# The attention mixers' task order taken from a table, and two weight splits of the Strassen stages issued earlier

## The chip, the core and the metric

One core of a Trainium2 chip runs the program. Its engines are TensorE (PE: matmuls and transposes, with weight loads that overlap them), VectorE (DVE), ScalarE (ACT), GpSimd (POOL) and SyncE (SP, which issues most of the DMAs). Each engine works through its own instructions in the order in which they were issued and waits at semaphores for the others. The metric is the device time of one execution in microseconds (us); less is better.

## The reference, cut to what matters

One decoder layer on x of 512 x 1024 (float32):

```
h  = x + 1/2 * SwiGLU_1(RMSNorm(x))                    # 1024 -> 2816 -> 1024
u  = RMSNorm(h);  one projection u @ w_in (3992 columns): q, k, v, gates
A  = NSA attention, 8 heads: compressed + selected + sliding window 512
B  = sliding-window attention (window 128), 8 heads, with a sink per head
h  = h + w_out(sigmoid(gA) * (A @ w_branch_a) + sigmoid(gB) * (B @ w_branch_b))
h  = h + 1/2 * SwiGLU_2(RMSNorm(h));   out = RMSNorm_final(h)
```

The compressed keys and values of NSA come from a small network: blocks of 32 tokens, 2048 -> 256, a tanh-GELU, 256 -> 64. With 512 tokens the selection takes all blocks of 64, so the selected branch is dense causal attention here.

## The kernel before, in words

**Numbers.** Each float32 operand is kept as two parts, a rounded high half and the rest as a low half, and a product is three matmuls (high x high, high x low, low x high). A weight block of 1024 x 128 is loaded by SP into a ring of raw tiles (`raw`, 4 deep) and split: `W.high`, line 160, copies the high half on ACT (`whi`), `W.low`, line 164, subtracts on DVE or POOL (`wlo`). The halves live in a ring of 4 slots, so a block's split may start when the block four places ahead is no longer read. `W.next()` hands out a block and first calls `W.prep` for the block two places on; `W.prep(n)` issues load and split of all blocks up to n that are still to be done.

**Stages.** First feed-forward part, mixers (about 387 to 652 us of the span), merge of the two branches and `w_out`, second feed-forward part. Instructions are issued to each engine in the order of the Python code, except in the mixers.

**The mixers.** Their work is 1123 tasks, made by `plan.add` and numbered in the order of their making. A task says which engine may run it and for how long by the planner's estimate (`us`; some have two engines, DVE or POOL), what it comes after, and which buffers it takes from a ring and gives back. `Schedule.run` is a list scheduler: it always issues the task that could start first by its own clocks, and so chooses the order on all engines and, for tasks with two engines, the engine. Fillers are projections and gate matmuls that keep PE at work between the attention's steps. Attention goes unit by unit: scores on PE (`s`), masked minimum on DVE (line 1261), exponentials on ACT (1269), reciprocal of the sum on DVE (1279), weighing of the probabilities on DVE or POOL (1290, 1292), transposes on PE (1355, `tp`), their two halves on ACT and DVE (1367, 1370), product with the values on PE (`o`).

At two places of the stage the tasks' numbers are needed; a p behind a number says POOL. Around 451 to 457 us the list scheduler issues

```
183 518 515 208 185 519 210 551 209 203 212 211 204 214 205 213 184 206 215 520 186 248 187 250
249p 521 216 252 217 532 254 251p 547 218 207 188 219
```

183, 515, 519, 551, 203 to 206 and 216 are PE's. 183 ends a projection of keys and values, 185 and 186 are its rotary products and their addition (line 893), 187 is the low half of its values (`v_low`, line 940), which frees the `acc` bank that 216, the first step of the next projection, takes. 209, 211, 213 and 215 are halves of splits (line 164). Around 474 to 490 us it issues

```
581 586 572 561 239 256 269 240 257 271 258 270p 259 273 558 275 272p 228 260 559 562 309 261 582
311 274p 563 313 277 315 262 278 276p 229 230 564 587 310p 573 263 279 231 574 280 264 312p 583
565 281 314p 265 575 588 584 603 266 316p 589 576
```

Here 239 ends a projection, 240 is its rotary products on DVE; 256 to 259 are the second half of the values' compression on PE; 260 adds its halves, 261 sums them on PE, 262 is the polynomial of the GELU (lines 1095 to 1098, DVE), 263 the tanh (ACT), 264 the product (lines 1105 and 1106, DVE), 265 the second matrix on PE. 581, 586 and 603 are scores of the window attention (0.48 us by the planner's formula), 282 is a step of a projection (0.725), 565 a sum of two halves of an attention output (line 1398, 0.84), 241 a rotary addition. 270, 272, 274, 276, 310, 312, 314 and 316 are halves of splits.

**The second feed-forward part.** 22 column blocks f in thirds of 8, 8 and 6. For each f there are two products, `pg` and `pu`, of 24 matmuls each; `gated` then forms silu(pg) * pu. In the first two thirds every odd f closes a pair, and `gated` goes on to form the seven sums that Strassen's scheme wants of the pair (lines 1503 to 1510), in their two halves. After a third, `down()` runs 14 steps of 12 matmuls (`STEPS`); each takes its weight block by `W.next()`, and each reads one of the seven sums, of the first two pairs (g = 0) or the last two (g = 1). The first four steps are (1, 0), (5, 0), (2, 0) and (1, 1); their banks are `acc`, `o`, `s` and `acc`. When `down()` begins, the blocks of the first two steps are split already, and that of the third is issued by the first step's `W.next()`.

Of the kernel before, what the change touches and what calls it, by code (L numbers as in the profile page):

```python
# [27 lines left out]
NEVER = 1e9  # L28
# [27 lines left out]
def f32(ap):  # L56
    return ap.bitcast(F32)


class Weights:  # L60
# [6 lines left out]
    def __init__(self, tc, ctx):  # L67
        self.nc = tc.nc
        self.raw_pool = ctx.enter_context(tc.tile_pool(name="wraw", bufs=self.RAW))
        pool = ctx.enter_context(tc.tile_pool(name="wring", bufs=1))  # L70
        self.hi = pool.tile([128, self.SLOTS, 8, 128], F32R, name="whi")
        self.lo = pool.tile([128, self.SLOTS, 8, 128], F32R, name="wlo")
        self.tc = tc
        self.blocks, self.wide = [], []
        self.stored = {}
        self.raw = []
        self.apart = {}
        self.prepped = 0
        self.pos = 0
# [109 lines left out]
    def next(self):  # L189
        i = self.pos  # L190
        self.prep(i + self.AHEAD)
        self.pos += 1
        return self.place(i)
# [25 lines left out]
    return dram(w, r0 * width + c0, [[width, 128], [128 * width, nk], [1, n]])  # L219


class Ring:


# [15 lines left out]
class Task:  # L240


    def __init__(self, us, emit, take, give, rank):
        self.us, self.emit, self.take, self.give, self.rank = us, emit, take, give, rank
        self.left, self.next, self.ready, self.sources = 0, [], 0.0, []


class Schedule:
# [10 lines left out]
    def add(self, us, emit, after=(), take=(), give=(), rank=0):  # L259

        t = Task(us, emit, take, give, rank)
        t.seq = len(self.tasks)
        for p in after:
            if p is not None:
                t.left += 1
                p.next.append(t)
        self.tasks.append(t)
        return t

    def delay(self, source, engine):  # L270
        return 0.0 if source == engine else self.SEM[source] + (self.TO_POOL if engine == "pool" else 0.0)

    def run(self):
        ready = [t for t in self.tasks if t.left == 0]
        for _ in self.tasks:
            best = None
            for t in ready:
                at = t.ready
                for ring, _ in t.take:
                    at = max(at, ring.ready())  # L280
                for e, us in t.us.items():
                    start = max(at, self.clock[e], self.port if "pool" in t.us else 0.0, *(end + self.delay(p, e) for p, end in t.sources))
                    key = (start, t.rank, us, t.seq)
                    if best is None or key < best[0]:
                        best = key, t, e, start + us
            _, t, e, end = best
            assert end < NEVER
            for ring, key in t.take:
                ring.take(key)
            for ring, key in t.give:  # L290
                ring.give(key, end)
            self.clock[e] = end
            if "pool" in t.us:
                self.port = end
# [11 lines left out]
def layer(ctx, tc, a, out):  # L306
# [5 lines left out]
    W = Weights(tc, ctx)  # L312
# [399 lines left out]
    with ExitStack() as mixing:  # L712
# [66 lines left out]
        plan = Schedule(act=3.0, dve=5.0)  # L779
# [3 lines left out]
        PREP, FILL, FETCH = -2, 9000, 5.0  # L783
        engine = {"dve": vector, "pool": gpsimd}
        fill = [None]
        used, prepped = {}, {}

        def task(engines, emit, after=(), **kw):
            if isinstance(engines, tuple):
                engines = {engines[0]: engines[1]}  # L790
            return plan.add(engines, emit, [x for x in after if x is not None], **kw)

        def either(us, more=0.06):

            return {"dve": us + more, "pool": 2 * us + 0.1}

        last_low = [None]

        def prepare(first, n):

            for half in range(2):
                for i in range(first, first + n):
                    if i in W.stored:
                        if half == 0:
                            prepped[i, 0] = prepped[i, 1] = task(("sp", FETCH), lambda i=i: W.fetch(i),
                                                                 (used.get(i - W.SLOTS),), rank=PREP)
                        continue
                    if i < W.prepped:
                        prepped[i, half] = None
                        continue  # L810
                    nk = W.blocks[i][1] // 2
                    k = slice(half * nk, half * nk + nk)
                    us = nk * 128 / 960 + 0.07
                    t = task(("act", us + 0.04), lambda i=i, k=k: W.high(i, k.start, k.stop), (used.get(i - W.SLOTS),),
                             rank=PREP)

                    def low(e, i=i, k=k, half=half):
                        W.low(i, k.start, k.stop, engine[e])
                        if half:
                            W.load(i + W.RAW)  # L820

                    x = prepped[i, half] = task(either(us, 0.12), low, (t, last_low[0] if half else None), rank=PREP)
                    if half:
                        last_low[0] = x

# [581 lines left out]
        nsa_count, swa_turns = [0], []  # L1407
        attend([*swa_units(0), *swa_units(1), *nsa_units(0), *nsa_units(1, (3, 2, 1, 0))])
        plan.clock["sp"] = plan.clock["store"] = 0.0
        plan.run()  # L1410
        W.pos = pos[0]
        W.prepped = pos[0] + 2
        att_stack.close()
# [50 lines left out]
    with pool("temp3", 2) as temp, pool("end") as end:  # L1464
# [18 lines left out]
        def gated(pg, pu, j, pairs):  # L1483
            z = temp.tile([128, S], F32, name="z")
            vector.tensor_tensor(z, pg, r_b, op=OP.mult)
            s = temp.tile([128, S], F32, name="s")
            scalar.activation(s, z, AF.Silu)
            t = temp.tile([128, S], F32, name="t")
            vector.tensor_tensor(t, pu, r_b, op=OP.mult)
            if not pairs:  # L1490
                g = temp.tile([128, 8, 256], F32, name="g").rearrange("p m c -> p (m c)")[:, :S]
                vector.tensor_tensor(g, s, t, op=OP.mult)
                split(G[:, j], G[:, 8 + j], g)
                return
            if j % 2 == 0:
                left["g"] = temp.tile([128, 8, 256], F32, name="g")
            g, p = left["g"], j // 2
            o = g[:, 1:3] if j % 2 else g[:, 0:8:7]
            vector.tensor_tensor(o, *(x.rearrange("p (i c) -> p i c", i=2) for x in (s, t)), op=OP.mult)
            if j % 2 == 0:  # L1500
                return
            hi, lo = left_hi[:, p], left["lo"][:, p]
            vector.tensor_tensor(g[:, 3], g[:, 7], g[:, 2], op=OP.add)
            scalar.copy(hi[:, 0:4], g[:, 0:4])
            vector.tensor_tensor(g[:, 4], g[:, 3], g[:, 0], op=OP.subtract)
            vector.tensor_tensor(lo[:, 0:4], g[:, 0:4], f32(hi[:, 0:4]), op=OP.subtract)
            vector.tensor_tensor(g[:, 5], g[:, 0], g[:, 7], op=OP.subtract)
            vector.tensor_tensor(g[:, 6], g[:, 1], g[:, 4], op=OP.subtract)
            scalar.copy(hi[:, 4:7], g[:, 4:7])
            vector.tensor_tensor(lo[:, 4:7], g[:, 4:7], f32(hi[:, 4:7]), op=OP.subtract)  # L1510
# [96 lines left out]
        for third, (f0, f1) in enumerate(THIRDS):  # L1607
            for f in range(f0, f1):
                pg = acc(False)
                mm3(pg, W.next(), u_in, KD, col if f == 0 else None)  # L1610
                pu = acc(False)
                mm3(pu, W.next(), u_in, KD, rows if f == 0 else None)
                if f < 2:
                    for d in range(4 * f, 4 * f + 4):
                        residual(d)
                if f == 1:
                    make_room()
                if third == 2:
                    next(last)
                gated(pg, pu, f - f0, third < 2)  # L1620
            if third < 2:
                down()
# [27 lines left out]
```

## Time and profile before

| | |
|---|---|
| median of 3 runs | 1136.74 us (1136.02 to 1137.89) |
| profiled execution, its own time | 1138.52 us |
| its span, first to last instruction | 1136.8 us |
| mean granted TensorE clock | 0.992 |
| PE busy | 1111.3 us, 98% of the span |
| DVE busy | 706.3 us, 62% |
| ACT busy | 472.0 us, 42% |
| POOL busy | 130.0 us, 11% |

Busy time of PE is the union of the matmuls' drawn lengths. Matmuls overlap in the pipeline: one of 256 columns is drawn 0.28 us long, and the next starts 0.12 us after it, so a short gap does not show as idle time. A granted clock of 1.00 is 2.4 GHz, 0.50 is 1.2 GHz. A row's bracket gives the idle time of the engine just before the instruction and what ended it; where an instruction waits for several things, the row names the one that came last by the profile, which can be another than the one that counted. "L164" is line 164 of the kernel before.

### The profile page before, as it was taken

The page shows a single profiled execution, that of the slowest core. Times are in us where ns is not written, and L with a number is a line of the kernel's source. Part 1 is how long each engine was busy: PE and PEld are TensorE (multiplying, and loading weights), DVE is VectorE, ACT ScalarE, POOL GpSimd, SP SyncE. Part 2 cuts the span into 40 slices and gives each one's busy share as a digit, 9 for nine tenths or more (in the row PEclk, how much of TensorE's full clock was granted, in tenths as well). Part 3 has the DMA queues.
Part 4 walks back from the last instruction along what each step waited for, and adds up shares of the span by engine and source line. Part 5 has one row for each costly group of instructions (what it writes and reads, how often), then busy time and mean ns, then how long its engine had stood idle before and what let it go on. Part 6 is the DMA issues. An engine that isn't in the chain of part 4 may idle for free.

```text
span 1136.8 us, 14825 instructions
## 1 busy us (share of the span) xinstructions
PE 1111.3 (98%) x5535; PEld 934.6 (82%) x5535; DVE 706.3 (62%) x1311; ACT 472.0 (42%) x887; POOL 130.0 (11%) x133
## 2 busy tenths in 40 slices
PE   7999999999999999989999999999999999999997
PEld 6888888888888999888888888788887888778875
DVE  4665447674656588888888645553656754675553
ACT  4443223321324457566666534443334322342332
POOL 0100000000002132731101233220000000000001
PEclk9999999999999999999999999999999999999999
DMA  7377657886734542224333245633243633264211
GB/s 228 93 240 227 199 165 241 286 275 212 241 125 140 147 111 76 75 75 144 116 122 111 88 144 165 169 99 87 84 126 120 189 85 101 75 195 138 82 67 74
DMA packets 201904, 163.16 MB, mean 144 GB/s; under 512 B 6820, under 2 KB 177384, under 8 KB 201832
## 3 DMA queue, kind: packets, MB, share of 16 engines
q1 hardware_dynamic: 199304, 158.00, 45.4%
q10 hardware_dynamic: 2528, 4.22, 1.0%
q8 instruction: 43, 0.70, 0.2%
q14 instruction: 29, 0.24, 0.1%
HBM read 133.88 MB, written 28.31 MB: 143 GB/s over the span
## 4 chain that ended last, share of the span: by engine, by line
PE 86%; DVE 5%; ACT 3%; DMA 2%; POOL 2%; issue 1%; SPq 0%; POOLq 0%; ACTq 0%; DVEq 0%
PE acc L328 34%; PE o L328 24%; PE s L328 24%; PE tp L1355 2%; DMA z<-zd 2%; DVE wlo L164 2%; POOL z L1453 1%; ACT whi L160 1%; POOL z L1431 1%; DVE s L1261 0%; PE tp L328 0%; DVE ml L332 0%; ACT mh L331 0%; DVE h L598 0%; ACT turn_a L516 0%
## 5 line engine op out<-in xcount | busy, mean ns | idle before, releaser
L164 DVE TENSOR_TENSOR wlo<-raw,whi 128x1024 fp32r<-128x1024 f32 (+2 forms) x194 | 214.3, 1136 | 33.2 <-ACT whi L160 33.1
L160 ACT CAST whi<-raw 128x1024 fp32r<-128x1024 f32 (+2 forms) x214 | 188.7, 917 | 98.0 <-PE acc L328 36.0
L328 PE MATMUL acc<-uh,whi 128*128 128x512 f32 x336 | 133.1, 396 | 0.0
L328 PE MATMUL acc<-ul,whi 128*128 128x512 f32 x336 | 131.3, 391 | 0.0
L328 PE MATMUL acc<-uh,wlo 128*128 128x512 f32 x336 | 131.2, 391 | 0.0
L328 PE MATMUL o<-uh,whi 128*128 128x512 f32 x264 | 104.3, 395 | 0.7 <-ACT uh L650 0.7
L328 PE MATMUL o<-ul,whi 128*128 128x512 f32 x264 | 103.2, 391 | 0.0
L328 PE MATMUL o<-uh,wlo 128*128 128x512 f32 x264 | 103.0, 390 | 0.0
L328 PE MATMUL s<-uh,whi 128*128 128x512 f32 x232 | 90.7, 391 | 0.0
L328 PE MATMUL s<-ul,whi 128*128 128x512 f32 x232 | 90.5, 390 | 0.0
L328 PE MATMUL s<-uh,wlo 128*128 128x512 f32 x232 | 90.5, 390 | 0.0
L328 PEld LDWEIGHTS acc<-uh,wlo 128*128 128x128 f32 x336 | 63.2, 188 | 14.0 <-DVE wlo L164 0.4
L328 PEld LDWEIGHTS acc<-ul,whi 128*128 128x128 f32 x336 | 63.3, 188 | 11.9
L328 PEld LDWEIGHTS acc<-uh,whi 128*128 128x128 f32 x336 | 63.3, 188 | 11.9
L328 PE MATMUL acc<-whi,uh 128*128 128x256 f32 x224 | 65.3, 292 | 2.0 <-DVE v L940 2.0
L328 PE MATMUL acc<-wlo,uh 128*128 128x256 f32 x224 | 64.1, 286 | 0.0
L328 PE MATMUL acc<-whi,ul 128*128 128x256 f32 x224 | 64.0, 286 | 0.0
L517 POOL TENSOR_TENSOR sqacc<-sqacc,turn_a 128x512 f32<-128x512 f32 x14 | 18.3, 1304 | 362.9 <-ACT turn_a L516 362.9
L328 PEld LDWEIGHTS o<-uh,whi 128*128 128x128 f32 x264 | 49.8, 189 | 11.9 <-ACT uh L650 1.1
L331 ACT CAST G<-g 128x512 fp32r<-128x512 f32 x28 | 17.4, 622 | 101.5 <-DVE g L569 72.3
L328 PEld LDWEIGHTS o<-uh,wlo 128*128 128x128 f32 x264 | 49.7, 188 | 10.6
L328 PEld LDWEIGHTS o<-ul,whi 128*128 128x128 f32 x264 | 49.9, 189 | 10.4
(339 smaller groups left out, 2306.3 us busy)
## 6 DMA issues: line engine op xcount, KB each, us to landing
raw<-in_ffn_gate_dram SPq DMA_DIRECT2D x42, 512.0 KB, 4.1
raw<-in_ffn_up_dram SPq DMA_DIRECT2D x42, 512.0 KB, 5.3
raw<-in_ffn_down_dram SPq DMA_DIRECT2D x34, 512.0 KB, 4.3
raw<-in_w_in_dram SPq DMA_DIRECT2D x20, 512.0 KB, 4.9
eraw<-in_ffn_down_dram SPq DMA_DIRECT2D x16, 512.0 KB, 6.5
raw<-t SPq DMA_DIRECT2D x16, 512.0 KB, 3.2
eraw<-in_w_in_dram SPq DMA_DIRECT2D x12, 512.0 KB, 7.1
early<-ehi SPq DMA_DIRECT2D x12, 512.0 KB, 5.2
```

What stands on the lines that cost most here:

```text
L160: self.nc.scalar.copy(self.place(i)[0][:, k0:k1], self.raw[i][:, k0:k1])
L164: engine.tensor_tensor(lo, self.raw[i][:, k0:k1], f32(hi), op=OP.subtract)
L328: tensor.matmul(out, lhsT, rhs, start=start, stop=stop)
L331: scalar.copy(hi, src)
L517: gpsimd.tensor_tensor(sqacc, sqacc, sq, op=OP.add)
L1355: tensor.transpose(ps[:w, hd], u.p[:, hd, kb * w:kb * w + w], ident)
L1431: gpsimd.tensor_tensor(z, z, r_b, op=OP.mult)
L1453: gpsimd.tensor_tensor(y, y, z, op=OP.add)
```

## The change

`Schedule` gets a second way to issue its tasks: `follow` reads a table, `ORDER`, with the numbers of all 1123 tasks in the order in which they are to be issued, with a p behind those that go to POOL. The tasks themselves are as before; that the second half of a split comes after the first half of the same block is now written down as a condition. In the second feed-forward part `W.prep` is called twice more at the end of each of the first two thirds: for the block of `down()`'s third step ahead of `gated` of the last f, and for that of the fourth step inside it, behind the product and ahead of the pair's sums. The diff, with the table cut to its first and last line and the two places named above:

```diff
+ORDER = """
+    0 1 2 3 4 5 6 7 14 15 16 10 11p 13 17 32 8 18 36 33 19 37 20 9 21 34 12 44 38 40 80 48 35 41 49 42 23 22 50 39p
...
+    513 528p 516 181 174 517 514 182 183 531 518 185 208 210 212 209 211 213 546 184 515 203 519 187 186p 204 205
+    214 551 520 206 547 216 521 217 248 215p 218 249p 188 252 192 219 220 250 253p 552 522 548 193 221 532 189 254
...
+    226 540 541 569 542 555p 236 570 543 237 227 238 571 544 545 556 557 560 239 572 561 256 269 240 257 258 271
+    270p 273 558 581 259 309 586 313 228 275 260 562 559 272p 261 311 274p 277 582 229 278 262 563 230 564 231 587
+    276p 263 279 280 565 312p 281 241p 310p 573 583 603 264 282 574 588 265 584 314p 283 608 266 604 267 605 284
+    585p 268 290 291 315 316p 566 285 567p 589 292 575 609 610 606 576 242 286 243p 577 293 294 288 295 611 296 578
...
+    458 473 474 475 476 477 478 479 468 1122p 480 469
+"""
...
-        self.left, self.next, self.ready, self.sources = 0, [], 0.0, []
+        self.left, self.next, self.after, self.ready, self.sources = 0, [], [], 0.0, []
...
                 p.next.append(t)
+                t.after.append(p)
...
+    def follow(self, order):
+
+        done = set()
+        for word in order.split():
+            t = self.tasks[int(word.rstrip("p"))]
+            e = "pool" if word[-1] == "p" else next(iter(t.us))
+            assert all(p in done for p in t.after) and all(ring.ready() < NEVER for ring, _ in t.take)
+            for ring, key in t.take:
+                ring.take(key)
+            for ring, key in t.give:
+                ring.give(key, 0.0)
+            done.add(t)
+            t.emit(e) if len(t.us) > 1 else t.emit()
+        assert len(done) == len(self.tasks)
...
-                    x = prepped[i, half] = task(either(us, 0.12), low, (t, last_low[0] if half else None), rank=PREP)
+                    x = prepped[i, half] = task(either(us, 0.12), low, (t, *((last_low[0], prepped[i, 0]) if half else ())), rank=PREP)
...
-        plan.run()
+        plan.follow(ORDER) if ORDER.strip() else plan.run()
...
             if j % 2 == 0:
                 return
+            if j == 7:
+                W.prep(W.pos + 3)
             hi, lo = left_hi[:, p], left["lo"][:, p]
...
                 if third == 2:
                     next(last)
+                if third < 2 and f + 1 == f1:
+                    W.prep(W.pos + 2)
                 gated(pg, pu, f - f0, third < 2)
```

Against the list scheduler's order no task of PE moves by more than 8 places among PE's own 444. 54 tasks change between DVE and POOL:

| kind of task | DVE to POOL | POOL to DVE |
|---|---|---|
| weighing of probabilities (1290, 1292) | 27 | 1 |
| low half of a split (164) | 7 | 2 |
| rotary addition (893) | 5 | 1 |
| low half of an attention output (1403) | 3 | 3 |
| low half of queries (972) | 2 | 1 |
| low half of the compression's input (1059) | 0 | 2 |

## Rows read from the trace of the kernel before

**Rows 1.** The page, part 1: busy us (share of span) xinstructions.

```profile
PE 1111.3 (98%) x5535; PEld 934.6 (82%) x5535; DVE 706.3 (62%) x1311; ACT 472.0 (42%) x887; POOL 130.0 (11%) x133
```

**Rows 2.** Waits of PE: line waited for, us in total, times, longest us.

```profile
PE tp L328 <- ACT pbuf L1269: 3.0, 1, 3.0
...
PE s L328 <- ACT whi L160: 2.6, 2, 1.3
...
PE o L328 <- DVE wlo L164: 1.4, 2, 0.9
```

**Rows 3.** Timeline of PE: start us, us, instruction, [idle before <- what ended it].

```profile
456.60 0.55 PE L328 MATMUL acc<-whi,uh 128*128 128x256 f32 x1 [2.03 <-DVE v L940]
```

**Rows 4.** Windows: length, busy PE, PEld, DVE, ACT, POOL, clock, DMA share, GB/s.

```profile
500.00:652.60 152.60, 152.26 (x885) 129.75 (x884) 123.84 (x380) 99.14 (x303) 26.14 (x34) 1.00 0.36 120
...
487.27:490.68 3.41, 3.41 (x16) 3.09 (x15) 3.24 (x13) 1.36 (x5) 2.53 (x3) 0.50 0.02 7
866.15:869.56 3.41, 3.41 (x10) 2.63 (x9) 2.63 (x3) 0.81 (x1) 0.00 (x0) 0.50 0.83 226
```

**Rows 5.** Timeline of PE, second Strassen stage: the first four steps' starts.

```profile
986.99 0.39 PE L328 MATMUL acc<-whi,G 128*128 128x512 f32 x1
...
989.76 0.39 PE L328 MATMUL o<-whi,G 128*128 128x512 f32 x1
...
994.01 0.50 PE L328 MATMUL s<-whi,G 128*128 128x512 f32 x1 [1.31 <-ACT whi L160]
...
995.27 0.50 PE L328 MATMUL s<-wlo,G 128*128 128x512 f32 x1 [0.54 <-DVE wlo L164]
...
999.21 0.42 PE L328 MATMUL acc<-whi,G 128*128 128x512 f32 x1
```

**Rows 6.** Timeline of PE, first Strassen stage: starts of steps one and four.

```profile
857.15 0.39 PE L328 MATMUL acc<-whi,G 128*128 128x512 f32 x1
...
869.26 0.54 PE L328 MATMUL acc<-whi,G 128*128 128x512 f32 x1
```

**Rows 7.** Timeline of DVE at the start of the second Strassen stage.

```profile
987.19 0.69 DVE L1489 TENSOR_TENSOR t<-o,r_b 128x512 f32<-128x512 f32 x1 [4.75 <-PE o L328]
987.98 0.69 DVE L1499 TENSOR_TENSOR g<-s,t 128x512 f32<-128x512 f32 x1
...
993.04 0.96 DVE L1510 TENSOR_TENSOR left<-g,G 128x768 fp32r<-128x768 f32 x1 [0.90 <-ACT G L1509]
993.99 4.63 DVE L164 TENSOR_TENSOR wlo<-raw,whi 128x1024 fp32r<-128x1024 f32 x4
```

**Rows 8.** Timeline of ACT at the same place.

```profile
992.91 3.88 ACT L160 CAST whi<-raw 128x1024 fp32r<-128x1024 f32 x4
```

**Rows 9.** Timeline of DVE ahead of the wait at 456.6.

```profile
452.04 2.48 DVE L164 TENSOR_TENSOR wlo<-raw,whi 128x512 fp32r<-128x512 f32 x4
454.44 1.49 DVE L893 TENSOR_TENSOR turn_a<-turn_a,turn_b 128x256 f32<-128x256 f32 x1
455.85 0.60 DVE L940 SCALAR_TENSOR_TENSOR v<-acc,rcol,v 128x128 fp32r<-128x128 f32 x2
```

**Rows 10.** Timeline of PE at the second long wait of the mixers.

```profile
486.83 0.65 PE L328 MATMUL tp<-w,sqacc 128*32 128x64 f32 x8 [3.02 <-ACT pbuf L1269]
```

**Rows 11.** Timeline of DVE ahead of that wait.

```profile
480.18 1.15 DVE L1096 TENSOR_TENSOR sqacc<-sqacc 128x128 f32<-128x128 f32 x1
...
486.44 0.29 DVE L1106 SCALAR_TENSOR_TENSOR sqacc<-sqacc 128x128 f32<-128x128 f32 x1
```

**Rows 12.** Line 1096: duration ns min/median/max, first and last start us, form.

```profile
L1096 DVE TENSOR_TENSOR sqacc<-sqacc x2: 291/718/1146, 437.3 to 480.2; 128x128 f32<-128x128 f32 x2
```

**Rows 13.** Timeline of POOL over the same stretch.

```profile
474.88 10.12 POOL L164 TENSOR_TENSOR wlo<-raw,whi 128x512 fp32r<-128x512 f32 x8 [3.97 <-ACT whi L160]
```

**Rows 14.** Groups of POOL by shape, 385:660: busy us, mean ns, idle before.

```profile
L1292 POOL TENSOR_SCALAR pbuf<-pbuf,c,gate 128x384 f32<-128x384 f32 x6 | 4.0, 668 | 26.4 <-DVE c L1279 12.1 <-PE acc L328 11.9 <-PE tp L1355 2.4
```

**Rows 15.** Groups of DVE by shape in the same stretch.

```profile
L1292 DVE TENSOR_SCALAR pbuf<-pbuf,c,gate 128x384 f32<-128x384 f32 x10 | 4.8, 480 | 0.5
```

More of the change, by code (lines that the diff above doesn't have):

```diff
@@ L219, in cols @@
     return dram(w, r0 * width + c0, [[width, 128], [128 * width, nk], [1, n]])
+ORDER = """
+    0 1 2 3 4 5 6 7 14 15 16 10 11p 13 17 32 8 18 36 33 19 37 20 9 21 34 12 44 38 40 80 48 35 41 49 42 23 22 50 39p
+    24 26 51 52 25p 53 43p 27 86 54 84 55 45 64 29 82 65 46 30 66 81 85 83p 67 56 57p 68 69 28 31 47 58 87 70 71 59
+    72 88 93 95 94p 96 89 60 61 62 90 97 98 91 99 489 100 101 133 134 102 137 135 73 138 139 136 103 104 92 74 63
+    140p 105 490 106 75p 502 107 503 108 117 78 491 109 118 76 119 77 492 504 110 507 120 111 493 121 112 122 505 79
+    494 506 495 123 496 113 124 155 157 524 115 161 508 141 142 114 125 497 156p 525 143 159 158p 160p 144 163 145
+    498 195 162 146 164 126 199 147 509 526 165 166 197 196p 200 116 167 168 198p 148 510 169 170 149 150 127 499
+    176 128p 151 201 529 172 202p 129 500 173p 152 177 130 131 178 511 153 175 154 179 171 132 512 501 527 180 530
+    513 528p 516 181 174 517 514 182 183 531 518 185 208 210 212 209 211 213 546 184 515 203 519 187 186p 204 205
+    214 551 520 206 547 216 521 217 248 215p 218 249p 188 252 192 219 220 250 253p 552 522 548 193 221 532 189 254
+    549 190 523p 251 207 194 222 553 191 223 255p 232 233 533 534 550p 538 234 554 224 535 568 225p 536 539 537 235
+    226 540 541 569 542 555p 236 570 543 237 227 238 571 544 545 556 557 560 239 572 561 256 269 240 257 258 271
+    270p 273 558 581 259 309 586 313 228 275 260 562 559 272p 261 311 274p 277 582 229 278 262 563 230 564 231 587
+    276p 263 279 280 565 312p 281 241p 310p 573 583 603 264 282 574 588 265 584 314p 283 608 266 604 267 605 284
+    585p 268 290 291 315 316p 566 285 567p 589 292 575 609 610 606 576 242 286 243p 577 293 294 288 295 611 296 578
+    590 244 607 579 246 245 297 360 247 298 591 580 317 595 592 612 299 625 630 318 301 596 287p 289 300p 593 319
+    597 626 302 303 594 306 598 304 307 627 599 305 308 320 613 631 321 614 349 617 618 322 632 600 615 619 323 601
+    324 616 602 628 620 325 333 621 334 335 629p 622 633 336 623 326 337 634 338 327 339 635 340 328p 636 329 624p
+    350 637 371 330 341 639 640 331 647 342p 332 638 343 641 642 648 656 351 344p 352 657 353 345 643 644 354 649
+    347 650 346 665 355 658 651 652 666 348 677 659 356 357 682 653 654 667 660p 668 678 661 645 358 662 655 361 669
+    670 663 362 363 664 671 683 672 679 695 684 680 696 364 365 697 685 646p 700 366 701 681p 367 698 686p 687 673
+    359 702 368 674 703 713 393 725 691 699p 714 369 688 372 675 689 692 693 373 726 690 370 382 704p 715 705 716
+    706 707 730 727 676 694 374 728 729p 709 735 717 708 710 375 711 731 718 719 712 732 376 720 740 736 721 737 741
+    733 742 377 722 378 738 757 743 379 739p 758 762 380 734p 759 763 383 384 744p 767 760 745 764 768 746 749 404
+    765 772 761p 750 747 385 386 769 770 753 415 748 751 723 754 724p 789 771p 773 752 755 387 774 790 801 756 791
+    775 802 766p 806 388 776p 777 781 807 389 803 778 811 390 782 381 792 779 808 785 783 780 812 391 784 804 805p
+    786 793 392 809 813 787 794 394 814 815p 810p 795 816 837 817 788 796 838 395 426 396 797 818 798 397 842 819
+    820 839 843 840 847 799 848 800p 821 822 825 398 841p 826 823 399 844 849 829 824 852 827 828 830 833 834 845
+    873 400 853 850 854 851p 831 835 832 401 874 846p 855 836 875 856p 885 405 857 406 858 876 859 861 407 865 862
+    886 890 860 863 887 866 891 867 869 402 864 888 870 408 871 892 877 895 868 900 896 409 893 897 872 901 921 898
+    902 410 878 903 922 411 923 879 926 412 894p 924 416 880 899p 417 904p 931 889 881 905 909 927 882 925p 932 928
+    936 906 418 910 419 413 907 911 929 908 930p 933 883 934 913 937 448 914 917 915 912 957 918 420 919 916 437
+    935p 938 969 939 958 403 970 421 974 940p 941 920 975 959 960 942 945 971 946 422 943 423 979 949 972 947 976
+    977 944 980 950 951 948 984 978p 953 981 427 985 952 982 954 986 961 428 962 1001 429 955 983p 1006 987 956 884p
+    988p 963 964 1002 424 973p 1003 965 989 1007 1011 990 430 993 966 1008 991 1012 425 994 1009 431 997 992 998
+    1013 432 1016 995 996 1033 1004 999 433 967 1005p 434 1017 1018 1010p 1014 1034 1035 1045 1015p 1019 1020 459
+    1000 1021 1025 968p 1046 1036 1022 1026 438 1023 439 1050 1029 1024 1047 414 1030 1027 1051 1037 1048 1031 1028
+    1052 440 1053 1032 1049p 1063 441 1054p 1038 1039 1064 1040 442 1068 435 1041 1065 1042 1055 1069 1056 1059 443
+    1060 1066 1070 1057 1061 444 1081 1058 445 1082 481 1093 1067p 449 1071 1083 1072p 1102 1073 1043 1077 1094 1095
+    450 451 1084 1062 1103 1074 1096 485 1044p 452 1097p 1078 1075 1111 1085 1104 1079 1112 1105 436 1076 1086 1087
+    1106p 1113 1080 1098 453 454 455 1088 1107 446 456 482p 1114 1089 1099 1108 483 1109 460 470 461 462 463 464
+    1100 1090 465 1101 1091 1092p 457 486p 466 1115 1110 447 467 1116 487 471 1117 1118 472 1119 484p 488p 1120 1121
+    458 473 474 475 476 477 478 479 468 1122p 480 469
```

## The prediction

> **What bounds the kernel now.** I read the page's busy line first, then TensorE's waits, then the granted clock by stretches, and last the timelines around each long wait. TensorE (PE) is busy 98% of the span [rows 1], so time can only be won where it stands still, or where it runs below its full clock. The table of waits is short [rows 2]. Four waits matter here: 3.0 us once (`tp`, in the mixers), two of 1.3 us for the high half of a weight (the third step of each `down()`), and one of 2.03 us for an `acc` bank [rows 3]. The 0.9 us wait of `o` for `wlo` lies ahead of the planned tasks and is not touched.
>
> Each of the four costs more than its idle time. After each stands a stretch of 3.41 us with the granted clock at 0.50, that is 1.2 instead of 2.4 GHz; two of the four stand in [rows 4], and in both PE is busy for all 3.41 us. Half clock over 3.41 us loses 1.7 us of work.
>
> **The splits in the Strassen stages.** In the second stage, step one starts at 986.99 and step two at 989.76, so a step is 2.77 us [rows 5]. Step four should start at 986.99 + 3 x 2.77 = 995.30 and starts at 999.21: 3.91 us lost. In the first stage it should start at 857.15 + 8.31 = 865.46 and starts at 869.26: 3.80 us lost [rows 6]. Together 7.7 us, the first wait (1.31 us), the second (0.54) and the half clock included.
>
> The cause is the order on VectorE (DVE) and ScalarE (ACT). The third step's block is split inside `next()` of the first step, behind all that `gated` issues for the last pair. DVE begins that pair's last operation, L1510, at 993.04 and only then four `wlo` in a row [rows 7]; ACT begins its four `whi` at 992.91 [rows 8], when PE has been ready since 986.99 + 2 x 2.77 = 992.53.
>
> The change issues that split ahead of `gated`, and the fourth step's between the product L1499 and the pair's sums. A split is 3.88/4 = 0.97 us on ACT and 4.63/4 = 1.16 us on DVE [rows 8, 7].
>
> - The first moved split needs the slot of the last `f`'s gate block, free when those matmuls end. DVE then sits idle for 4.75 us ahead of L1489 [rows 7]. The split, 0.97 + 1.16 = 2.1 us, goes into that hole, and behind it `z`, as long as L1489, and the Silu. It costs nothing; without that cover, up to 1.2 us.
> - The second needs the slot of the up block, free at 987.0. ACT copies it by 988.2, while DVE does L1489 and L1499. Its low half then pushes the pair's chain on DVE back by about 1.2 us: L1510 ends at 993.04 + 0.96 + 1.2 = 995.2, before step four begins at 995.3, and that step reads earlier terms. What is late next is the fifth step's split, at 995.2 + 1.16 = 996.4, wanted at 998.1. No new wait.
> - The loads behind these splits move forward with them on SP's queue. Nothing else stands in that queue there.
>
> Gain: 7.7 us; bounds 7.2 (a few tenths left over) and 7.9.
>
> **The table in the mixers.** All 1123 tasks remain. PE's order changes little: no PE task moves by more than 8 places. 44 tasks go from DVE to GpSimd (POOL), 10 come back; 27 of the 44 are weighings (L1290, L1292), 26 of them after 500 us. Where can that pay? Between 500 and 652.6 us PE idles 152.60 - 152.26 = 0.34 us [rows 4], so little is to be won there. What is to be won lies at two places.
>
> *The wait at 456.6.* PE's task 216 needs an `acc` bank, which 187 (`v_low`, L940) frees. On DVE 187 stands behind four splits (2.48 us) and 186, an addition of 1.49 us, and starts at 455.85 [rows 9]. The table gives the fourth split (215) and 186 to POOL and puts 187 right behind the third split: 452.04 + 3 x 0.62 + 0.60 = 454.5. PE issues the same tasks ahead of 216 as before and would come to it at 456.60 - 2.03 = 454.6. The wait goes, or is up to 0.6 us if POOL's addition holds DVE up (half of a POOL split of twice the columns, 10.12/8 = 1.27 us, [rows 13]). I take 0.4. Without a long wait I expect no fall of the clock: gain 2.03 - 0.4 + 1.7 = 3.3 us; bounds 1.4 (0.6 left, and the fall) and 3.7.
>
> *The wait at 486.8.* The row names an ACT operation [rows 10], but PE's 265 reads the product L1106, which DVE ends at 486.44 + 0.29 = 486.73 [rows 11]. Slow ahead of it are small operations on SBUF: L1096 took 0.291 us at the first compression and 1.146 us at this one [rows 12]. All through it POOL runs eight `wlo` back to back [rows 13]. Such an operation of DVE here waits for the POOL operation to end. The table keeps POOL's splits there and moves another POOL addition (241) in among them, so that loss stays. What it does is to give PE more to do first: 581, 586, 603 and 282 now stand between 239, which starts the chain on DVE, and 265: 3 x 0.48 + 0.725 = 2.2 us by the program's own costs. Against that 565 (0.84 us by its cost) now stands ahead of the product on DVE. The wait becomes 3.02 - 2.2 + (0 to 0.84) = 0.8 to 1.7 us; I take 1.3, a gain of 1.7 us. Whether the clock still falls is open: after the 0.9 us of [rows 2] it did not, after 1.31 and 0.54 it did. I count the fall as staying. Bounds of the gain: 1.3 and 4.7 (no wait, no fall).
>
> *The rest.* A weighing of 384 columns takes 0.67 us on POOL and 0.48 us on DVE [rows 14, 15]; three have 128 columns, which POOL did not run here: above nothing and below 0.67 us, I take 0.5. From the sums to the transposes the chain gets longer by some tenths each time, and gate matmuls run in between. New waits of PE: at best none, at worst those of the slower rival; I take 0.5 us.
>
> The rows show what POOL does to DVE: 0.291 us become 1.146 us [rows 12]. The Trainium skill, SBUF — State Buffer, section "Who interferes with whom", says that a DVE operation with two SBUF inputs and a POOL operation that reads SBUF take turns on one port, the later one blocked until the other ends; the trace agrees. The Trainium skill, Perfetto Trace Analysis, section "Optimizing Scalar/DVE Operations", adds that moving work between those two engines may therefore not help; by that the mixers' term would be 0 and not 4.5 us.
>
> Sum: 7.7 + 3.3 + 1.7 - 0.5 = 12.2 us. Against the profiled execution's own 1138.52 us that is 1126.3; that execution lies 1.8 us above the median of the runs, 1136.74, from which the sum gives **1124.5 us**.
>
> **The rivals.**
>
> - *Both mixer waits and both falls go.* 7.7 + 3.7 + 4.7 + 0.3 = 16.4: 1120.3. For it: 2.2 us of cover come near 3.02. Against: the held-up operations stay. Gaps that are too short for the table of waits could add a little.
> - *POOL's part takes back what the mixers win.* The added POOL work (weighings of 0.67 us, splits of 1.27 us) holds DVE up at other places, as at 480; new waits of PE eat the 4.5 us. Only the Strassen part is left: 1129.0. Against: after 500 us DVE is busy 123.84 of 152.60 us [rows 4] and gives away 26 x 0.48 = 12.5 us of it or more.
> - *Slower.* Transposes wait for the 26 weighings after 500 us, which end later on POOL. If PE stood still for each, the 12.7 us (the sum without the 0.5) would be gone from 0.49 us a piece on. At 0.67 us, a whole POOL operation, it is 17.4 - 12.7 = 4.7 us slower: 1141.4. Against: PE idles 0.34 us there now, and the gate matmuls fill.
> - *The moved splits do nothing*, since their slot or their data come late: 12.2 - 7.7 = 4.5, 1132.2. Against: the 4.75 us of DVE's idle time.
>
> **How the numbers follow.** Forecast 0.53 (1122 to 1127 around 1124.5), both waits gone 0.20, taken back by POOL 0.18, splits without effect 0.05, slower 0.04. To leave out no more than 2 in 10 the range goes from below the second case, 1118.5, to above the third, 1130. A change of 0.2% (2.3 us) is about what a measurement of this kernel can tell from none. Faster needs below 1134.5: all cases but the last and a little of the fourth, 0.94; same 0.03; slower 0.03.
>
> **What would show it.** Right: no wait of `s` for `whi` L160 and no granted 0.50 in either `down()`, four steps in a row at 2.77 us; no wait for L940 near 455; a wait of about 1 us left ahead of the second compression's second product, with L1096 still near 1.1 us there; DVE's busy time lower by 15 to 25 us, POOL's higher by 20 to 35. Wrong: new waits of PE for POOL's `pbuf` or `wlo`, a third step that waits for `wlo`, or a clock that falls at a new place.

## The result and the profile after

The changed kernel takes 1126.07 us, median of 4 runs (1124.65 to 1127.99), beside 1136.79 us for the kernel before; the ratio is 0.9911, 95% interval 0.989 to 0.9932. That is 10.7 us faster; forecast were 12.2. The profiled execution took 1127.99 us, its span is 1126.0. In two of the experiments below one run each took far longer (1576 and 1852 us, at a mean granted clock of 0.66 and 0.56) and is left out of the medians given.

The busy line of the page after. Code lines lie 64 further down than before (L328 is now L392, L940 is L1004, L1096 is L1160); in the experiments with an edited table they lie 62 further down.

```profile
PE 1104.4 (98%) x5535; PEld 930.7 (83%) x5535; DVE 688.9 (61%) x1264; ACT 472.4 (42%) x887; POOL 163.7 (15%) x180
```

Against [rows 1] DVE has 17.4 us less and POOL 33.7 us more, both inside what was forecast. PE's waits after (line waited for, us in total, times, longest); two longer ones, for data at the program's start, stand ahead of these:

```profile
...
PE o L392 <- DVE wlo L164: 1.4, 2, 0.9
PE acc L392 <- ACT whi L160: 1.2, 1, 1.2
PE s L392 <- ACT whi L160: 1.0, 1, 1.0
...
PE tp L1045 <- DVE ql L1036: 0.5, 1, 0.5
```

The 3.0 us of [rows 2] are gone, and with them the two waits of 1.3 us in the Strassen stages: the `s` that waits for `whi` here stands at 714.72, in the merge of the branches. The first steps of both Strassen stages, timeline of PE after:

```profile
854.29 0.39 PE L392 MATMUL acc<-whi,G 128*128 128x512 f32 x1
...
862.61 0.39 PE L392 MATMUL acc<-whi,G 128*128 128x512 f32 x1
...
980.15 0.39 PE L392 MATMUL acc<-whi,G 128*128 128x512 f32 x1
...
982.93 0.39 PE L392 MATMUL o<-whi,G 128*128 128x512 f32 x1
...
985.70 0.39 PE L392 MATMUL s<-whi,G 128*128 128x512 f32 x1
...
988.48 0.39 PE L392 MATMUL acc<-whi,G 128*128 128x512 f32 x1
```

Four steps in a row at 2.77 us, with no wait. From step one to step four it is 8.32 us in the first stage, where it was 869.26 - 857.15 = 12.11 [rows 6], and 8.33 in the second, where it was 12.22 [rows 5]: 3.79 + 3.89 = 7.68 us won. DVE in the second stage shows the two moved splits (at 975.82 and 981.76) and the end of the pair's chain:

```profile
975.82 1.23 DVE L164 TENSOR_TENSOR wlo<-raw,whi 128x1024 fp32r<-128x1024 f32 x1 [2.58 <-ACT whi L160]
...
980.36 0.69 DVE L1553 TENSOR_TENSOR t<-o,r_b 128x512 f32<-128x512 f32 x1 [2.71 <-PE o L392]
...
981.76 1.22 DVE L164 TENSOR_TENSOR wlo<-raw,whi 128x1024 fp32r<-128x1024 f32 x1
...
987.23 0.96 DVE L1576 TENSOR_TENSOR left<-g,G 128x768 fp32r<-128x768 f32 x1 [0.90 <-ACT G L1575]
```

The hole ahead of L1489, 4.75 us before [rows 7], has shrunk by 2.04 us to 2.71 (it now stands ahead of L1553): the first moved split has taken its place there and delays nothing. The pair's last operation ends 8.04 us after step one's start; forecast were 995.2 - 986.99 = 8.2.

Windows of after (columns as in [rows 4]):

```profile
455.00:500.00 45.00, 42.75 (x354) 41.22 (x353) 41.56 (x121) 30.67 (x90) 28.26 (x26) 1.00 0.27 77
500.00:652.60 152.60, 151.85 (x873) 129.99 (x872) 103.79 (x326) 98.74 (x301) 54.99 (x78) 1.00 0.35 117
840.00:1000.00 160.00, 160.00 (x702) 131.61 (x701) 104.64 (x131) 58.77 (x66) 0.00 (x0) 1.00 0.42 131
```

The clock is 1.00 in all three, where before it was at 0.50 four times for 3.41 us. DVE gave away 20.05 us between 500 and 652.6, and PE's idle time there rose from 0.34 to 0.75 us. What is left, and what is new, in PE's timeline:

```profile
444.17 0.42 PE L392 MATMUL tp<-w,sqacc 128*64 128x64 f32 x4 [0.73 <-issue]
...
457.95 0.35 PE L392 MATMUL acc<-whi,uh 128*128 128x256 f32 x1 [1.25 <-ACT whi L160]
...
484.01 0.74 PE L392 MATMUL s<-ks_t,G 128*128 128x256 f32 x4 [0.78 <-ACT pbuf L1333]
...
485.68 0.61 PE L392 MATMUL tp<-w,sqacc 128*32 128x64 f32 x8 [0.22 <-issue]
...
648.11 0.50 PE L392 MATMUL acc<-uh,whi 128*128 128x512 f32 x1 [0.68 <-ACT turn_a L1236]
```

457.95 is the old wait at 456.6 [rows 3], 484.01 and 485.68 are what is left of the one at 486.8 [rows 10]; 444.17 and 648.11 are new, as is the 0.5 us for `ql` (a low half of queries) at 416.8 in the table of waits. Of the last two of these places, only the 0.22 us stand ahead of the product's matmuls; the 0.78 us stand ahead of the scores 603, which wait for a bank of `s` and were meant as cover for the chain. The row at 457.95 names ACT, whose split ends within 0.01 us of `v_low` on DVE (457.21 + 0.59 = 457.80). That `v_low` is again what PE waits for is seen from two runs below: with one moved split the same wait (1.26 us) names L1004, and without POOL at this place it is gone. DVE and POOL ahead of it, two timelines of after:

```profile
454.36 2.93 DVE L164 TENSOR_TENSOR wlo<-raw,whi 128x512 fp32r<-128x512 f32 x2
457.21 0.59 DVE L1004 SCALAR_TENSOR_TENSOR v<-acc,rcol,v 128x128 fp32r<-128x128 f32 x2
```

```profile
453.99 1.05 POOL L957 TENSOR_TENSOR turn_a<-turn_a,turn_b 128x256 f32<-128x256 f32 x1 [3.89 <-DVE turn_b L942]
455.10 4.57 POOL L164 TENSOR_TENSOR wlo<-raw,whi 128x512 fp32r<-128x512 f32 x3
```

Two splits took 2.93 us on DVE, where four had taken 2.48 [rows 9]: POOL's addition 186 and then its split 215 held one up each. And the second compression's polynomial on DVE, under POOL's splits as before [rows 11 to 13]:

```profile
479.05 1.11 DVE L1160 TENSOR_TENSOR sqacc<-sqacc 128x128 f32<-128x128 f32 x1
480.19 1.19 DVE L1161 TENSOR_SCALAR sqacc<-sqacc 128x128 f32<-128x128 f32 x1
481.42 1.29 DVE L1162 TENSOR_TENSOR sqacc<-sqacc 128x128 f32<-128x128 f32 x1
...
484.72 0.46 DVE L1169 TENSOR_SCALAR sqacc<-sqacc 128x128 f32<-128x128 f32 x1
```

L1169 is L1105 of before, the first operation of the product, which is not shown in [rows 11]. DVE of before:

```profile
485.03 1.30 DVE L1105 TENSOR_SCALAR sqacc<-sqacc 128x128 f32<-128x128 f32 x1
```

Before, POOL's addition 241 ran beside it, which the table now issues earlier; after, the end of a split. With POOL taken away, in a run below, it takes 0.23 us.

### The profile page after: what moved, and what is told of

Read it like the earlier page. It is cut to its first block, busy times and chain, and to the rows that moved or that the text cites. A ratio compares the mean times of both kernels' runs of the same rounds, so it can differ in the third digit from the quotient of the medians.

```text
span 1126.0 us, 14867 instructions
## 1 busy us (share of the span) xinstructions
PE 1104.4 (98%) x5535; PEld 930.7 (83%) x5535; DVE 688.9 (61%) x1264; ACT 472.4 (42%) x887; POOL 163.7 (15%) x180
## 4 chain that ended last, share of the span: by engine, by line
PE 86%; DVE 5%; ACT 3%; DMA 2%; POOL 2%; issue 1%; SPq 0%; POOLq 0%; DVEq 0%; ACTq 0%
PE acc L392 34%; PE o L392 24%; PE s L392 24%; PE tp L1419 2%; DMA z<-zd 2%; DVE wlo L164 2%; POOL z L1517 1%; ACT whi L160 1%; POOL z L1495 1%; DVE turn_a L1117 0%; DVE ml L396 0%; PE tp L392 0%; ACT mh L395 0%; DVE h L662 0%; ACT turn_a L580 0%
## 5 line engine op out<-in xcount | busy, mean ns | idle before, releaser
L392 PE MATMUL acc<-uh,whi 128*128 128x512 f32 x336 | 133.6, 398 | 0.7 <-ACT turn_a L1236 0.7
L392 PE MATMUL acc<-uh,wlo 128*128 128x512 f32 x336 | 131.5, 391 | 0.0
L392 PE MATMUL acc<-ul,whi 128*128 128x512 f32 x336 | 131.3, 391 | 0.0
L392 PE MATMUL o<-uh,whi 128*128 128x512 f32 x264 | 104.3, 395 | 0.6 <-ACT uh L714 0.6
L392 PE MATMUL o<-uh,wlo 128*128 128x512 f32 x264 | 103.2, 391 | 0.0
L392 PE MATMUL o<-ul,whi 128*128 128x512 f32 x264 | 103.2, 391 | 0.0
L392 PE MATMUL s<-uh,whi 128*128 128x512 f32 x232 | 90.7, 391 | 0.0
L392 PE MATMUL s<-ul,whi 128*128 128x512 f32 x232 | 90.6, 390 | 0.0
L392 PE MATMUL s<-uh,wlo 128*128 128x512 f32 x232 | 90.5, 390 | 0.0
L392 PEld LDWEIGHTS acc<-uh,wlo 128*128 128x128 f32 x336 | 63.2, 188 | 14.0 <-DVE wlo L164 0.4
L392 PEld LDWEIGHTS acc<-uh,whi 128*128 128x128 f32 x336 | 63.3, 188 | 12.9 <-ACT turn_a L1236 1.1
L392 PEld LDWEIGHTS acc<-ul,whi 128*128 128x128 f32 x336 | 63.3, 188 | 12.0
L392 PE MATMUL acc<-whi,uh 128*128 128x256 f32 x224 | 65.5, 292 | 1.2 <-ACT whi L160 1.2
L392 PE MATMUL acc<-wlo,uh 128*128 128x256 f32 x224 | 63.3, 283 | 0.1
L392 PE MATMUL acc<-whi,ul 128*128 128x256 f32 x224 | 63.3, 283 | 0.0
L395 ACT CAST G<-g 128x512 fp32r<-128x512 f32 x28 | 17.4, 622 | 101.4 <-DVE g L633 72.3
L392 PEld LDWEIGHTS o<-uh,whi 128*128 128x128 f32 x264 | 50.0, 189 | 11.8 <-ACT uh L714 1.0
L392 PEld LDWEIGHTS o<-uh,wlo 128*128 128x128 f32 x264 | 49.8, 189 | 10.6
L392 PEld LDWEIGHTS o<-ul,whi 128*128 128x128 f32 x264 | 49.9, 189 | 10.5
```

The lines of the kernel that those rows point to most:

```text
L392: tensor.matmul(out, lhsT, rhs, start=start, stop=stop)
```

## The experiments

Each was timed beside the kernel before, whose medians were 1136.56 us (the first four runs below), 1136.74 (the next four) and 1138.06 (the last four). Numbers in the table's edits are tasks; a p sends one to POOL.

**One part alone.** The moved splits with the list scheduler's tasks, and the table with both new calls of `W.prep` taken out:

```diff
-        plan.follow(ORDER) if ORDER.strip() else plan.run()
+        plan.run()
```

> The two moved splits alone; the mixers are issued by the list scheduler as before. Theory (the parts add up): the third step of each down() no longer waits, 3.9 + 3.8 us are won, 1136.8 - 7.7 = 1129.1 us; the mixers' waits of 2.0 and 3.0 us and their two falls of the clock stay. Rival (the moved splits only shift the wait to a later step): a new wait of about 1 us in each stage, 1132 to 1134 us.

```diff
-            if j == 7:
-                W.prep(W.pos + 3)
...
-                if third < 2 and f + 1 == f1:
-                    W.prep(W.pos + 2)
```

> The table alone; the splits stay behind gated. Theory (the parts add up): what the whole change won, 10.7 us, less the 7.7 us of the splits: 3 us, 1133.8 us; the two waits and falls of the clock in the Strassen stages stand as before. Rival (the table wins more by itself and loses it in the merge only together with the splits): 1131 us or less.

The splits alone gave 1129.90 us, ratio 0.9944 (0.9923 to 0.9965); the table alone 1132.03, 0.9964 (0.9949 to 0.9979). Gains of 6.7 and 4.5 us, 11.2 together, where the whole change gave 10.7: the parts add up, within the spread of the runs. PE's timeline with the splits alone, and a window behind its second row:

```profile
456.53 0.36 PE L392 MATMUL acc<-whi,uh 128*128 128x256 f32 x1 [2.03 <-DVE v L1004]
...
486.78 0.61 PE L392 MATMUL tp<-w,sqacc 128*32 128x64 f32 x8 [3.03 <-ACT pbuf L1333]
```

```profile
487.56:490.97 3.41, 3.41 (x16) 3.22 (x16) 3.24 (x14) 1.51 (x6) 2.56 (x3) 0.50 0.02 5
```

Both mixer waits stand there untouched, with their falls of the clock; of the Strassen loss nothing is left (8.32 us from step one to step four in both stages). With the table alone the Strassen waits are those of before, in both stages, but the clock is not. Timeline of PE and windows at the second stage:

```profile
980.78 0.39 PE L392 MATMUL acc<-whi,G 128*128 128x512 f32 x1
...
987.80 0.51 PE L392 MATMUL s<-whi,G 128*128 128x512 f32 x1 [1.31 <-ACT whi L160]
...
989.06 0.50 PE L392 MATMUL s<-wlo,G 128*128 128x512 f32 x1 [0.52 <-DVE wlo L164]
...
991.46 0.39 PE L392 MATMUL acc<-whi,G 128*128 128x512 f32 x1
```

```profile
986.00:991.00 5.00, 3.17 (x13) 1.97 (x12) 4.17 (x4) 4.60 (x5) 0.00 (x0) 1.00 0.17 64
991.00:996.00 5.00, 5.00 (x23) 4.07 (x22) 2.79 (x4) 2.16 (x4) 0.00 (x0) 1.00 0.96 312
```

The waits of 1.31 and 0.52 us are followed by no fall. Step one to step four takes 10.68 us here and not 12.22: the same late split costs 2.35 us in this execution and 3.9 in the profiled one of before.

**Half of the table.** The table's order with the list scheduler's engines, and the list scheduler's order with the table's engines; the splits stay moved in both.

```diff
 # the table's order, p only where the list scheduler chose POOL; at 457
-... 187 186p 204 205 214 ... 215p 218 249p ...
+... 187 186 204 205 214 ... 215 218 249p ...
 # the list scheduler's order, p as in the table; at 457
+... 184 206 215p 520 186p 248 187 250 249p ...
```

> The table's order and the moved splits, but each task on the engine that the list scheduler chose (the 44 tasks back on DVE, the 10 back on POOL). Theory (the order wins, not the move to POOL): 187 still stands ahead of 186 and 215, PE still has 2.2 us more to do ahead of 265, so both mixer waits stay short and the time is that of the changed kernel, 1125 to 1127 us; the wait near 457 could even go, since POOL no longer holds the two splits ahead of 187. Rival (DVE's relief wins): the waits come back, 1129 us or more.

> The list scheduler's order and the moved splits, but with the table's choice of DVE or POOL for each task. Theory (the order wins): 187 stands where it stood, but 186 and 215 are off DVE, so the wait at 456.6 is halved at best, and the wait at 486.8 stays at 3 us with its fall of the clock: 1127 to 1129 us. Rival (DVE's relief wins): 1126 us or less.

1133.09 us, 0.9969 (0.9955 to 0.9982), and 1136.10, 0.9995 (0.9982 to 1.0008). Both are slower than the splits alone, by 3.2 and 6.2 us: my theory that the order does the work fell, and neither half is a gain. In the second the waits for `v_low` (1.72 us) and ahead of the second product (3.02) stay, and a new long one stands at 442, for a split behind the first compression's polynomial. PE, DVE and POOL of that run:

```profile
442.24 0.35 PE L390 MATMUL acc<-wlo,uh 128*128 128x256 f32 x1 [2.95 <-DVE wlo L164]
```

```profile
438.77 1.19 DVE L1158 TENSOR_TENSOR sqacc<-sqacc 128x128 f32<-128x128 f32 x1
```

```profile
433.54 7.54 POOL L164 TENSOR_TENSOR wlo<-raw,whi 128x512 fp32r<-128x512 f32 x6 [9.91 <-ACT whi L160]
```

Splits that the table sends to POOL lie, in the old order, back to back under that polynomial. In the first, `ql` comes late at 417.80 (2.12 us) behind a DVE split of 1.70 us, and the scores near 486 wait 1.77 us for their bank; the clock falls behind both.

**POOL taken away at a wait.** At 457 the addition and the fourth split go back to DVE, behind `v_low`; at 480 POOL's addition (241) and splits go behind the polynomial; and the bank that is emptied late at 648 is emptied first.

```diff
 # at 457
-... 187 186p 204 205 214 ... 215p ...
+... 187 214 186 215 204 205 ...
 # at 480
-... 312p 281 241p 310p ... 314p ... 316p ... 567p ...
+... 281 ... 567p 241p 312p 310p 314p 316p ...
 # at 648
-... 478 479 468 ...
+... 468 478 479 ...
```

> The changed kernel, but 186 and 215 back on DVE, right behind 187, so that POOL has nothing to read while DVE does the three splits ahead of 187. Theory (POOL's operations hold DVE up): the two splits that took 2.93 us take 1.3, 187 ends 1.6 us earlier, and PE's wait of 1.25 us near 458 goes; 1124.7 us. Rival (the two splits are slow for another reason, or DVE is short of time): they stay near 1.4 us each, and the added 1.3 us on DVE make the wait no shorter; 1126 us or more.

> The changed kernel, but POOL does the addition 241 and the splits 310, 312, 314 and 316 only behind 567, so that it stands still from about 480 to 486 us. Theory (POOL's operations hold DVE up): the two last of the three polynomial operations that take 1.1 to 1.3 us take 0.2 to 0.3, the chain to 265 is 2 us shorter, and PE's waits of 0.78 and 0.22 us go; 1125.1 us. Rival (the splits come too late for the projection behind, or the loads behind them do): a wait for a low half of a weight near 496 us, 1127 us or more.

> The changed kernel, but ACT empties the bank of the last but one gate block (468) ahead of that of the last one (479), as the list scheduler does. Theory (the table's swap of the two makes the wait of 0.68 us at 648): that wait goes, 1125.3 us. Rival (the bank that the merge takes first is the other one): the wait stays; 1126 us.

> The changed kernel with the three edits of the other runs of this set together. Theory: they add up, 1.4 + 1.0 + 0.8 = 3.2 us, 1122.9 us, unless a shorter wait at 458 only moves the next wait. Rival (the mixers' work on DVE and POOL sets the pace, and PE's waits come back elsewhere): 1125 us or more.

The first: 1124.28 us, 0.9893 (0.9874 to 0.9912), and the wait at 457.95 is gone. Its DVE, timeline:

```profile
452.87 1.89 DVE L164 TENSOR_TENSOR wlo<-raw,whi 128x512 fp32r<-128x512 f32 x3
454.67 0.60 DVE L1002 SCALAR_TENSOR_TENSOR v<-acc,rcol,v 128x128 fp32r<-128x128 f32 x2
```

Three splits at 0.63 us a piece without POOL beside them, and `v_low` 2.5 us earlier; that POOL holds DVE up there is shown. The second: 1130.03 us, 0.9943 (0.9923 to 0.9963), slower than the change. Its DVE, POOL and PE:

```profile
479.50 0.23 DVE L1159 TENSOR_SCALAR sqacc<-sqacc 128x128 f32<-128x128 f32 x1
479.76 0.29 DVE L1160 TENSOR_TENSOR sqacc<-sqacc 128x128 f32<-128x128 f32 x1
```

```profile
488.99 5.08 POOL L164 TENSOR_TENSOR wlo<-raw,whi 128x512 fp32r<-128x512 f32 x4
494.04 1.31 POOL L1034 TENSOR_TENSOR ql<-turn_a,ql 128x512 fp32r<-128x512 f32 x1
```

```profile
495.40 1.26 PE L1043 MATMUL tp<-ident_r,ql 128*128 128x128 f32 x8 [3.52 <-POOL ql L1034]
```

The mechanism held: 1.19 and 1.29 us became 0.23 and 0.29, and both waits near 484 are gone, that of the scores too. The time did not follow, because `ql` (task 243) now stands on POOL behind four delayed splits; PE waits 3.5 us for it, and 6.83 us at half clock come with it. The third: 1123.77 us, 0.989 (0.987 to 0.991), and the 0.68 us at 648 are gone. All three together, 1128.19, 0.993 (0.9912 to 0.9949), keep the 3.5 us.

**Edits that keep `ql` early.** To the edits at 457 and 648 come, in turn: at 480, splits 314 and 316 behind `ql` and not ahead of it; at the first compression, a low half of queries (128) and a split (198) go back to DVE, behind the polynomial and the product (task 127 moves up with them); and both. The edits at 457 and 648 were not run as a pair without a third, so what each run below adds to them is read from its waits and not from its time.

```diff
 # splits behind 243
-... 312p 281 241p 310p ... 314p ... 316p ... 567p ... 243p ...
+... 281 241p ... 567p 312p 310p ... 243p 314p 316p ...
 # first compression
-... 198p 148 ... 149 150 127 499 176 128p 151 ...
+... 148 ... 127 149 128 150 499 176 151 198 ...
```

> The two edits that won (186 and 215 on DVE behind 187; 468 ahead of 479), and at 480 only the splits moved: POOL does 312 and 310 behind 567 and 314 and 316 behind 243; the additions 241 and 243 keep their place. Theory (the 3.5 us wait of the earlier try came from 243 standing behind four splits, not from the splits): no wait near 495; one of the three polynomial operations is still held up by 241, two take 0.2 to 0.3 us; the waits of 0.78 and 0.22 us near 484 shrink to 0.3 together; 1122.5 us. Rival (the splits come too late): a wait for a low half near 496, 1125 us.

> The two edits that won, and at 440 the low halves 128 (queries) and 198 (a split) on DVE behind the product 149 and behind 151, so that POOL reads nothing while DVE does the polynomial and the product of the first compression. Theory (POOL holds DVE up there too, 1.35 and 1.31 us instead of 0.29): the wait of 0.72 us near 444 goes; 1122.5 us. Rival (the added 1.3 us on DVE delay what stands behind): a new wait between 444 and 456, 1123.5 us or more.

> All four edits together: 186 and 215, 468, the splits at 480, and 128 and 198. Theory: the waits near 444, 458, 484 and 648 are all gone or under 0.3 us, 1121.5 us, 4.5 us under the changed kernel. Rival: the waits come back elsewhere, 1123.5 us or more.

The first gave 1124.01 us, 0.9883 (0.9865 to 0.9901). The waits near 484 are gone, but another 0.7 us stands at 498, for `pts` (a half of the transposed probabilities) on DVE. DVE and POOL of that run:

```profile
490.70 4.44 DVE L1352 TENSOR_SCALAR pbuf<-pbuf,c 128x256 f32<-128x256 f32 x4
...
495.40 0.60 DVE L1352 TENSOR_SCALAR pbuf<-pbuf,c 128x256 f32<-128x256 f32 x2
```

```profile
491.61 2.64 POOL L164 TENSOR_TENSOR wlo<-raw,whi 128x512 fp32r<-128x512 f32 x2
```

Now four weighings on DVE, beside POOL's `ql`, these splits and an addition, take 1.11 us each, where the two later ones take 0.30 each with no POOL operation beside them: the hold-up has moved from the polynomial to them. The first compression's edit gave 1122.87, 0.9872 (0.9853 to 0.989), without the 0.73 us at 444. All edits together gave **1121.99 us** (1121.42 to 1122.9), 0.9867 (0.9849 to 0.9885): its runs all lie below those of the change (1124.65 at the least). It has the lowest median, but its runs overlap with those of the version before it (1121.62 at the least), and the 0.7 us for `pts` stay.

**One of the two moved splits.** The table, and the third step's split alone moved up:

```diff
-            if j == 7:
-                W.prep(W.pos + 3)
```

> The changed kernel without the second moved split: only the third step's is issued ahead of gated, the fourth's follows from next() as before. Theory (only the third step's split was late; the fourth's starts when the pair's chain ends at its old time, 994.0 in the trace of before, ends at 995.2 and is wanted at 995.3): no wait of 0.3 us or more in either stage, the time of the changed kernel, 1126 us. Rival (the fourth is late as soon as the third is on time): a wait of 0.5 to 1 us for a low half at the fourth step of each stage, 1127 to 1128 us.

1125.38 us, 0.9897 (0.988 to 0.9913), not to be told from the whole change, and its step four, too, comes without a wait. DVE of that run, whose step one starts at 977.73 and step four at 986.05:

```profile
984.74 3.50 DVE L164 TENSOR_TENSOR wlo<-raw,whi 128x1024 fp32r<-128x1024 f32 x3
```

With the third step's block out of the way, the first split here ends at 984.74 + 3.50/3 = 985.9, just before step four starts. The second move is worth nothing that these runs can measure.

## Why the prediction was right, and where it was not

| term | forecast, us | measured between the two profiled executions, us |
|---|---|---|
| splits in the Strassen stages | 7.7 | 7.68; as the gain of that part alone, by medians, 6.7 |
| wait at 456.6 | 3.3 | 2.03 - 1.25 + 1.7 = 2.5 |
| wait at 486.8 | 1.7 | 3.02 - 1.00 + 1.7 = 3.7 |
| new waits | -0.5 | -(0.5 + 0.73 + 0.68) = -1.9 |
| sum | 12.2 | 12.0, of which 10.5 came |

The mechanism was right in the main. That the sum comes out at 12.0 is in part luck: three terms of the mixers were off by 0.8, 2.0 and 1.4 us, and their errors nearly cancel.

- **The splits.** The cause, the hole on DVE and the chain of the pair were as forecast, to 0.2 us. Only the price of the falls is not fixed. Where they stay out, as in the run of the table alone, the two late splits cost (10.71 - 8.32) + (10.68 - 8.33) = 4.7 us. And the moved splits were not equally needed: with the third step's alone no wait is left.
- **The wait at 456.6** is the term whose size was wrong downwards. I took up to half of a POOL split for POOL's part. Two POOL operations came, one after the other, and each held a DVE split up: 2.93 us in place of 1.3. That the wait stays for this reason, the run without POOL there shows.
- **The wait at 486.8.** 1.3 us left, with L1160 near 1.1 us, was forecast, and 0.78 + 0.22 was found. The cover of 2.2 us came: between 239 and the product's matmuls PE worked 10.7 us (473.95 to 485.68, less 1.00 of waits), where it had worked 8.5 (475.05 to 486.83, less 3.24). The 0.84 us of 565 stand ahead of the product as forecast, but L1169 took 0.46 us there and not 1.30, which gives them back; the prediction held that POOL's loss stays whole, and here it did not. "I count the fall as staying" was the wrong choice of two: it did not come, and 1.7 us more were won. The other three runs of the change show the same granted clock as the profiled one, 0.998.
- **New waits**: 0.5 was too little. Two of the three named in the table were followed up and could be taken away: at 648 the order of two ACT tasks frees a bank late, and at 444 POOL again holds an operation of the polynomial (1.35 us) and one of the product (1.31) up; the edit to the first compression ends it. At 416.8 the cause was not tried.
- **From 12.0 to 10.5.** I summed, for each matmul, by how much the time to the next one's start exceeds the median for its shape. Between the profiled executions, 350 to 650 us fell from 21.3 to 17.3 and 850 to 1000 from 8.8 to 1.2. But 700 to 750 rose from 1.7 to 3.3, and the first 50 us from 7.4 to 8.1. In the run with one moved split, whose code in these two stretches is the same, they show 2.0 and 7.0: most of this belongs to the execution and not to the change. The sum also has a flaw of its own: it was read from an execution with all four falls (granted clock 0.992) and then taken off a median of runs that need not all have them. Of the 51 runs of the kernel before beside the experiments, only 18 were at 0.992.
- **The rivals.** That POOL takes back the mixers' part did not happen on the whole (4.5 us for the table alone, as forecast), though the single hold-ups are its mechanism. No wait of PE names a weighing on POOL; no run moved the weighings alone. The Trainium skill, Perfetto Trace Analysis, section "Optimizing Scalar/DVE Operations", says that work moved between DVE and POOL might not help. That agrees with the run of engines without order (6.2 us slower); the table (4.5 us faster) shows that it can help with an order made for it.

Two things stay open. No run shows how much of the mixers' gain each moved task brings. And emptying the bank at 648 first took 2.3 us off the median (1123.77 beside 1126.07) where the wait was 0.68 us; the rest may be the spread between runs and chips, and no run here tells it apart.

## What to carry to other kernels

When a wait ends on a split or a copy that an in-order engine issues behind other work, look for a hole on that engine ahead of that work and issue it there; then check one step further what is late next, since the second move may bring nothing. Here, moving work to GpSimd paid where no short VectorE operation on SBUF that TensorE waits for ran beside a split or an addition, so choose engine and order together. Take a fall of the clock as something that a wait may bring, not as part of its price.

## What the runs showed of the hardware

- **POOL beside DVE.** In the stretches shown here a DVE operation that reads two tensors from SBUF and starts under a split or an addition of POOL ends only behind it: the small ones 0.02 to 0.15 us after its end, a split of 512 columns 0.55. So 0.29 became 1.11 to 1.35 us, and a split of 0.63 became 1.46. Some operations with one tensor input wait too: L1161 took 1.19 us under POOL and 0.23 without, and the weighings of L1352 took 1.11 and 0.30; the reciprocal does not (L1343, 0.17 us under POOL's addition at 492.77 as elsewhere). Operations that read PSUM beside them kept their time (the copy ahead of the polynomial 0.28 us with POOL's splits running). The Trainium skill, SBUF — State Buffer, section "Who interferes with whom", calls the port pair that the two engines share an exclusive lock; the rows agree. But POOL's weighings did not hold L1342 up, which reads two tensors: it took 0.17 us under one and 0.84 under POOL's `ql`. DVE and POOL of after:

```profile
487.24 0.17 DVE L1342 TENSOR_TENSOR sum<-sum,e 128x2 f32<-128x2 f32 x1
...
491.99 0.84 DVE L1342 TENSOR_TENSOR sum<-sum,e 128x2 f32<-128x2 f32 x1
```

```profile
486.02 1.83 POOL L1354 TENSOR_SCALAR pbuf<-pbuf,c 128x256 f32<-128x256 f32 x2 [0.92 <-DVE c L1343]
...
491.52 1.30 POOL L1036 TENSOR_TENSOR ql<-turn_a,ql 128x512 fp32r<-128x512 f32 x1 [0.29 <-ACT ql L1033]
```

- **The clock.** The same waits (1.31 and some 0.53 us) were followed by 3.41 us at 0.50 in one execution and by none in another. The kernel before ran 51 times beside the experiments: at a granted clock of 0.997 it took 1133.4 to 1134.1 us (9 runs), at 0.992 1137.8 to 1140.4 (18 runs). So this kernel's time, with its four long waits, spreads over 7 us; the five runs of the version with all edits spread over 1.5. One of these five lists a granted clock of 0.948 and took 1122.9 us all the same, so a run's mean clock alone does not give its time.
